# A later product, a later start and fewer one-hots on TensorE in the expert stage of a streaming-encoder trunk

## The chip, the cores and the metric

The kernel runs on one core of a Trainium2 chip. The metric is device time in microseconds (us), the median of several runs. The engines are TensorE (PE in the rows, its weight loads PEld), VectorE (DVE), ScalarE (ACT), GpSimd (POOL) and SyncE (SP, which here only issues DMAs).

## The reference, cut to what matters

One layer: a convolution group and a state-space group side by side, then cross-attention to a memory, then PEER, and a final RMSNorm. There are 256 tokens of width 2048, in two tiles (tt = 0 and 1) of 128. Only PEER is touched:

```
s1, i1 = top_k(q1 . keys1, 16);  s2, i2 = top_k(q2 . keys2, 16)
idx, g = the 16 best of the 256 sums (s1 + s2), softmax over them   # 8 heads: 128 experts a token
act = gelu(einsum("td,tkd->tk", xt, u_tab[idx]))                    # the "curve" is this gelu
out = einsum("tk,tkd->td", g * act, v_tab[idx])                     # "the gates' product": g * act
```

There are 128 x 128 experts; an expert's number is 128 * i1 + i2.

## The kernel before

PEER's inner product over 2048 columns is split. For the last 1280 columns the rows of `u_tab` are gathered: `dot` (L925) issues one gather on GpSimd into one of five buffers (L928) and one multiply-and-sum on VectorE (L930, tile `u`), 128 for each token tile, 256 in all. For the first 768 columns TensorE scores all experts (`dense`, L960) into tables W[0] (tile WA) and W[1] (WB, read as `by_token`), and the 128 scores that a token needs are taken out of its table with one-hot matrices. That is **settling** (`settle`, L1086). It works on 32 groups of four tokens in each tile, tile 0 first:

- `onehots` (L992): eight small matmuls (L999, tile d) and two ScalarE relus (L1006) make one-hots E and H.
- `select` (L1010): y = table x E on TensorE (L1016 for tile 0, L1019 for tile 1).
- `pick` (L1023): VectorE multiplies H by y (L1026), and four matmuls add the columns up into `more` (L1028). A group is picked LAG = 3 (tile 0) or 2 (tile 1) groups after its one-hots.
- `finish` (L909), once a tile: ScalarE copies `more` (L911), TensorE adds the gathered and the dense part and turns them (L913 and L914, tile ptc), ScalarE takes the gelu (L915, tile cT), VectorE multiplies by the gates (L918: the product), TensorE turns it back (L920), ScalarE stores `coef` (L921).
- `left` and `build` (L1031, L1047): the table is written again, now with the coefficients. `left` makes dr (L1035) and a one-hot L, either by a matmul and a relu (L1043, L1044) or by an is_equal on VectorE (L1039). `build` makes R = relu(dr) x cT on VectorE (L1051), and four matmuls give pw (L1054), which ScalarE copies into the table (L1055). Tile 0's groups 0 to 27 are built while tile 1 is picked. Its last four and all 32 of tile 1 come behind that, in a tail (L1157 to L1163).

Then the V stage (L1202 to L1223) multiplies both tables with `v_tab`, 128 blocks of matmuls (tile acc).

VectorE's order is written by hand (L1122): a dot is written, then `Pace` advances `settle` by SETTLE_RATE = 2.2 steps, a step being the code up to the next `yield`. Settling starts ahead of dot number SETTLE_AT. TensorE and ScalarE are ordered by a scheduler, and each engine runs its queue in order. In the tail the scheduler orders VectorE too.

`finish` of tile 0 stands in `settle` at its place (L1112), so its two `yield`s on either side of the product are steps of `settle`: four steps, of which two lie ahead of the product.

Of the kernel before, what the change touches and what calls it, by code (L numbers as in the profile page):

```python
# [62 lines left out]
ROUTE_RATE = 4.0  # L63
DENSE_RATE = 0.8
SETTLE_RATE = 2.2
SETTLE_AT = 176
FEATS_AT = 150
LAG = (3, 2)
DELAY = 16
# [9 lines left out]
def trunk(ctx, tc, a, out, dbg=None):  # L79
# [3 lines left out]
    def bc(ap, shape):  # L83
        return ap.to_broadcast(shape)
# [64 lines left out]
    with ExitStack() as wctx:  # L149
# [71 lines left out]
        def run(g):  # L221
            for _ in g:
                pass
# [763 lines left out]
    def feats(route, g):  # L987
        return fe_at[route.tt][:, g % 8], C[:, g // 8]
# [3 lines left out]
    def onehots(route, g):  # L992
        psq, lr_q = settling_pools
        f, cs = feats(route, g)
        one = []
        for s, nm in ((1, "E"), (0, "H")):
            d = psq.tile([P, 4, P], F32, name="d")
            for i in range(4):
                PE.matmul(d[:, i, :], cs[:, i, :], f[:, s, :], start=i == 0, stop=i == 3, skip_group_check=True)  # L999
            if nm == "E":  # L1000
                x = lr_q.tile([P, 4, P], F32, name="E")
            elif route.tt and g % 3 == 2:
                x = spare_h
            else:
                x = lr_q.tile([P, 4, P], F32, name="H", tag="R" if route.tt == 0 and g % 4 > 1 else "H")
            S.activation(x, d, AF.Relu)  # L1006
            one.append(x)
        return one

    def select(route, g, E, H):  # L1010
        psq, lr_q = settling_pools
        y = psq.tile([P, 4, P], F32, name="y", tag="dr" if route.tt == 0 and g % 4 > 1 else "y")
        for i in range(4):
            t = 4 * g + i
            if route.tt == 0:
                PE.matmul(y[:, i, :], W[0][:, t, :], E[:, i, :], start=i == 0, stop=i == 3, skip_group_check=True)  # L1016
            else:
                for h in range(2):
                    PE.matmul(y[64 * h:64 * h + 64, i, :], by_token[:, h, t, :], E[:, i, :], start=i == 0, stop=i == 3,  # L1019
                              skip_group_check=True)  # L1020
        return H, y

    def pick(route, g, H, y):  # L1023
        if g == 0:
            route.more = psu.tile([P, NSLOT], F32, name="more", bufs=1)
        V.tensor_mul(H, H, y)  # L1026
        for i in range(4):
            PE.matmul(route.more[i * NQ:(i + 1) * NQ, :], onecol[:, NQ - g:2 * NQ - g], H[:, i, :], start=g == 0,  # L1028
                      stop=g == NQ - 1)

    def left(route, g):  # L1031
        psq, lr_q = settling_pools
        f, cs = feats(route, g)
        dr = psq.tile([P, 4, P], F32, name="dr")
        PE.matmul(dr, f[:, 0, :], cs, start=True, stop=True)  # L1035
        tag, bufs = ("L", 3) if route.tt == 0 or g % 2 else ("H", 2)
        L = lr_q.tile([P, 4, P], F32, name="L", tag=tag, bufs=bufs)
        if route.tt and g % 2:
            V.tensor_tensor(L, bc(iota[:, None, :P], [P, 4, P]), bc(route.gT[:, 1, 4 * g:4 * g + 4, None], [P, 4, P]),  # L1039
                            op=ALU.is_equal)  # L1040
        else:
            d = psq.tile([P, 4, P], F32, name="d")
            PE.matmul(d, f[:, 1, :], cs, start=True, stop=True)  # L1043
            S.activation(L, d, AF.Relu)  # L1044
        return dr, L

    def build(route, g, dr, L):  # L1047
        psq, lr_q = settling_pools
        ts = slice(4 * g, 4 * g + 4)
        R = lr_q.tile([P, 4, P], F32, name="R", tag="E" if route.tt and g % 2 else "R", bufs=2)  # L1050
        V.scalar_tensor_tensor(R, dr, 0.0, bc(route.cT[:, ts, None], [P, 4, P]), op0=ALU.max, op1=ALU.mult)  # L1051
        pw = psq.tile([P, 4, P], F32, name="pw", tag="y") if route.tt and g % 2 else psu.tile([P, 4, P], F32, name="pw")
        for i in range(4):
            PE.matmul(pw[:, i, :], L[:, i, :], R[:, i, :], start=i == 0, stop=i == 3, skip_group_check=True)  # L1054
        S.copy(W[route.tt][:, :, ts], pw.rearrange("p t b -> p b t"))  # L1055

    routes = [Route(0), None]
# [28 lines left out]
    def settle():  # L1086
        groups = P // 4
        ones_at, held = {}, {}
        for tt in range(NTT):
            lefts = []  # L1090
            lag = LAG[tt]
            for n in range(groups + lag):
                if n < groups and (tt, n) not in ones_at:
                    ones_at[tt, n] = onehots(routes[tt], n)
                if 0 < n <= groups:
                    held[tt, n - 1] = select(routes[tt], n - 1, *ones_at.pop((tt, n - 1)))
                yield
                if n >= lag:
                    pick(routes[tt], n - lag, *held.pop((tt, n - lag)))
                    yield  # L1100
                if tt:
                    if HOLD < n <= groups:
                        build(routes[0], n - HOLD - 1, *lefts.pop())
                    if HOLD <= n <= groups:
                        lefts.append(left(routes[0], n - HOLD))
                    yield
            if tt == 0:
                while tick[0] <= NSLOT:
                    yield
                for n in range(2):  # L1110
                    ones_at[1, n] = onehots(routes[1], n)
                yield from routes[0].finish()  # L1112
            else:
                held_left.append(lefts.pop())

# [9 lines left out]
    for tt in range(NTT):  # L1125
        for g in range(len(GROUPS[tt])):
            while (tt, g) not in ready:
                next(routing)
            h0, n = routes[tt].heads(g)
            for j in range(h0 * TOPK, (h0 + n) * TOPK):  # L1130
                if tick[0] == SETTLE_AT:
                    run(routing)
                    run(dense_gen)
                    for _, task in tasks:
                        run(task)
                    psd_x.close()
                    lr_d_x.close()
                    settling_pools += [
                        psx.enter_context(tc.tile_pool(name="psq", bufs=2, space=PSUM, reuse_waits="tile")),
                        lr_x.enter_context(tc.tile_pool(name="lr_q", bufs=2, side="right", reuse_waits="tile"))]  # L1140
                    load_feats(1)
                    settling = settle()
                    paces = [Pace(settling, SETTLE_RATE)]
                routes[tt].dot(j)
                tick[0] += 1
                for at, task in tasks:
                    if tick[0] >= at:
                        next(task, None)
                if tick[0] == FEATS_AT:
                    load_feats(0)  # L1150
                for p in paces:
                    p()
    run(settling)
    order.close()
    finishing = routes[1].finish()
# [3 lines left out]
    for i, (tt, g) in enumerate(todo):  # L1159
        now, ahead = ahead, left(routes[todo[i + 1][0]], todo[i + 1][1]) if i + 1 < len(todo) else None  # L1160
        if tt == 1 and g == 0:
            run(finishing)
        build(routes[tt], g, *now)  # L1163
# [108 lines left out]
```

## Time and profile before

| | us |
|---|---|
| runs, median (lowest to highest of 3) | 2059.61 (2057.92 to 2060.23) |
| the profiled execution's own time | 2058.54 |
| its span, first to last instruction | 2056.8 |
| TensorE busy, share of the span | 1960.9 (95%) |
| VectorE busy | 1681.5 (82%) |
| ScalarE busy | 999.4 (49%) |
| GpSimd busy | 786.2 (38%) |

The profiled execution took 1.07 us less than the median, and 1.7 us of it lie outside the span. The shares are means over stages with different limits. The stages that matter here, in us from the span's start: dots beside the dense scores to 1292, settling of tile 0 to 1361, of tile 1 to 1478, the tail to 1525, the V stage to 2038, the final norm to the end. A TensorE that is busy all the time may still be stretched, since the ends of matmuls are modelled.

### The profile page before, as it was taken

The numbers are of one execution on the slowest core, as the hardware profiler recorded it, in microseconds if no ns is written. First come the engines' busy times: TensorE is split into PE (matmuls) and PEld (weight loads), VectorE is DVE, ScalarE is ACT, GpSimd is POOL, SyncE is SP. The second block draws the span as 40 slices with busy tenths as digits, with TensorE's granted clock in tenths as the row PEclk, the third lists the DMA queues.
The fourth block names the chain that finished last, engine by engine and source line by source line (L and its number), as shares of the span: only waits on it lengthen the run. The fifth ranks groups of instructions, "written<-read, shape, count | busy, mean of one in ns | idle before, by whom it ended". The sixth has DMA issues, their size and how long they took to land.

```text
span 2056.8 us, 33321 instructions
## 1 busy us (share of the span) xinstructions
PE 1960.9 (95%) x12361; PEld 1682.5 (82%) x12379; DVE 1681.5 (82%) x2757; ACT 999.4 (49%) x1586; POOL 786.2 (38%) x589
## 2 busy tenths in 40 slices
PE   7899999998999999999999999989999999999996
PEld 7888886786899888888888878867678888888885
DVE  6699999895665557999976667888869899899998
ACT  5775765454644445333333323556554444444444
POOL 1011111000000004443446655453128777677775
PEclk9999999999999999999999999999999999999998
DMA  8888788857855567999999999988539999999996
GB/s 245 198 226 222 202 220 227 229 179 221 286 174 177 168 203 266 305 312 321 322 363 403 408 390 396 302 289 266 160 143 337 359 339 336 346 339 336 342 339 226
DMA packets 203108, 571.78 MB, mean 278 GB/s; under 512 B 31410, under 2 KB 39459, under 8 KB 202818
## 3 DMA queue, kind: packets, MB, share of 16 engines
q1 hardware_dynamic: 135810, 307.48, 44.4%
q0 software_dynamic: 67136, 262.18, 38.0%
q8 instruction: 97, 1.59, 0.3%
q14 instruction: 65, 0.53, 0.1%
HBM read 556.74 MB, written 12.85 MB: 277 GB/s over the span
## 4 chain that ended last, share of the span: by engine, by line
PE 56%; DVE 15%; issue 11%; DMA 8%; POOL 7%; ACT 1%; SPq 0%; POOLq 0%; DVEq 0%; ACTq 0%
PE acc L1220 8%; PE acc L1219 8%; PE acc L1218 8%; POOL u L928 7%; DVE u L930 5%; PE mm L216 4%; PE mm L215 4%; PE mm L214 4%; PE mm L206 3%; PE mm L207 3%; PE mm L205 3%; PE pw L1054 3%; DMA w_lo<-in_w_kv_mem 3%; PE y L1019 1%; DMA xc<-in_mem 1%
## 5 line engine op out<-in xcount | busy, mean ns | idle before, releaser
L1183 POOL DMA_INDIRECT v<-in_peer_v,vidx x256 | 394.1, 1539 | 180.9 <-DVE accg L1185 70.5
L930 DVE SCALAR_TENSOR_TENSOR u<-u,hnF 128x1280 f32<-128x1280 f32 x256 | 384.5, 1505 | 81.5 <-DMA u<-in_peer_u,uidx 79.5
L928 POOL DMA_INDIRECT u<-in_peer_u,uidx x256 | 300.3, 1173 | 324.3 <-DVE u L930 235.6
L978 PE MATMUL sy<-hnT,ut 128*128 128x256 f32 x1536 | 357.5, 385 | 13.4 <-ACT ut L974 12.4
L191 ACT CAST w_hi<-w_raw 128x1024 fp32r<-128x1024 f32 (+2 forms) x228 | 231.4, 1017 | 246.1 <-PE mm L207 116.0
L978 PEld LDWEIGHTS sy<-hnT,ut 128*128 128x128 f32 x1536 | 287.2, 193 | 54.7 <-ACT ut L974 16.3
L196 DVE TENSOR_TENSOR w_lo<-w_raw,w_hi 128x1024 fp32r<-128x1024 f32 (+2 forms) x192 | 227.4, 1186 | 112.9 <-ACT w_hi L191 110.7
L103 ACT CAST vh<-vr 128x1472 fp32r<-128x1472 f32 x128 | 183.1, 1431 | 251.5 <-PE acc L1219 167.9
L1219 PE MATMUL acc<-vh,wl 128*128 128x512 f32 (+1 forms) x768 | 295.4, 385 | 0.0
L1220 PE MATMUL acc<-vl,wh 128*128 128x512 f32 (+1 forms) x768 | 293.7, 385 | 0.2 <-DVE vl L104 0.2
L216 PE MATMUL mm<-aT_hi,w_lo 128*128 128x256 f32 x960 | 270.6, 289 | 17.9 <-DMA w_lo<-in_w_in 6.8
L1218 PE MATMUL acc<-vh,wh 128*128 128x512 f32 (+1 forms) x768 | 275.9, 384 | 2.4 <-ACT vh L103 2.4
L214 PE MATMUL mm<-aT_hi,w_hi 128*128 128x256 f32 x960 | 276.2, 290 | 0.3 <-ACT w_hi L191 0.3
L215 PE MATMUL mm<-aT_lo,w_hi 128*128 128x256 f32 x960 | 273.8, 287 | 0.0
L104 DVE TENSOR_TENSOR vl<-vr,vh 128x1472 fp32r<-128x1472 f32 x128 | 216.7, 1693 | 45.5 <-ACT vh L103 34.7
L1185 DVE SCALAR_TENSOR_TENSOR accg<-v,coef,accg 128x576 f32<-128x576 f32 x256 | 208.6, 815 | 4.1
L216 PEld LDWEIGHTS mm<-aT_hi,w_lo 128*128 128x128 f32 x960 | 181.9, 193 | 24.4 <-DMA w_lo<-in_w_in 8.0
L214 PEld LDWEIGHTS mm<-aT_hi,w_hi 128*128 128x128 f32 x960 | 185.0, 193 | 5.8 <-issue 3.7
L215 PEld LDWEIGHTS mm<-aT_lo,w_hi 128*128 128x128 f32 x960 | 185.4, 193 | 3.4 <-issue 2.0
L974 ACT COPY ut<-ut 128x768 f32<-128x768 f32 x128 | 100.4, 800 | 168.0 <-PE ut L972 143.8
L1219 PEld LDWEIGHTS acc<-vh,wl 128*128 128x128 f32 x768 | 144.5, 188 | 30.6 <-DVE wl L1209 0.4
L1218 PEld LDWEIGHTS acc<-vh,wh 128*128 128x128 f32 x768 | 144.7, 188 | 28.3 <-ACT vh L103 2.6
(385 smaller groups left out, 3233.3 us busy)
## 6 DMA issues: line engine op xcount, KB each, us to landing
vr<-in_peer_v SPq DMA_DIRECT2D x128, 736.0 KB
raw<-in_peer_u SPq DMA_DIRECT2D x127, 384.0 KB
w_raw<-in_w_kv_mem SPq DMA_DIRECT2D x64, 512.0 KB
w_raw<-in_w_in SPq DMA_DIRECT2D x48, 512.0 KB
w_raw<-in_w_out SPq DMA_DIRECT2D x32, 512.0 KB
w_raw<-in_w_q_mem SPq DMA_DIRECT2D x32, 512.0 KB
w_raw<-in_w_o_mem SPq DMA_DIRECT2D x32, 512.0 KB
w_lo<-in_w_kv_mem POOLq DMA_DIRECT2D x24, 512.0 KB
```

The costliest lines, as they stand in the source:

```text
L191: S.copy(hi, raw)
L196: V.tensor_sub(lo, raw, hi.bitcast(F32))
L214: PE.matmul(o, wh, ah, start=first and cb % 2 == 0, stop=False, skip_group_check=True)
L215: PE.matmul(o, wh, al, start=False, stop=False, skip_group_check=True)
L216: PE.matmul(o, wl, ah, start=False, stop=last and end, skip_group_check=True)
L928: G.indirect_dma_start(out=u, out_offset=None, in_=a["peer_u"].rearrange("e (q c) -> (e q) c", c=GU), in_offset=bass.IndirectOffsetOnAxis( ...
L930: V.scalar_tensor_tensor(u, u, 1.0, hnF[:, self.tt, :], op0=ALU.mult, op1=ALU.mult, accum_out=self.act[:, j:j + 1])
L978: PE.matmul(ps[:, b % 2, :], ut[:, k, :], hnT[:, k, :], start=k == 0 and b % 2 == 0, stop=k == KD - 1 and b % 2 == 1, skip_group_check=True)
L1183: G.indirect_dma_start(out=v, out_offset=None, in_=table, in_offset=bass.IndirectOffsetOnAxis(ap=vidx[tt][:, j:j + 1], axis=0))
L1218: PE.matmul(o, wh[:, tt, :], vh[:, cs_], start=b == 0, stop=False)
L1219: PE.matmul(o, wl[:, tt, :], vh[:, cs_], start=False, stop=False)
L1220: PE.matmul(o, wh[:, tt, :], vl[:, cs_], start=False, stop=b == NB - 1)
```

## The change

Three edits. (1) In `settle`, only the first part of tile 0's `finish` stays at its place; the rest (product, turn back, `coef`) is run at the start of step n = 3 of tile 1, and its four yields are no longer steps of `settle`. (2) SETTLE_AT goes from 176 to 179. (3) In `left`, the groups of tile 1 whose one-hot L is made on VectorE are those with g % 3 not 0 (21 of 32) in place of the odd ones (16 of 32).

```diff
-SETTLE_AT = 176
+SETTLE_AT = 179
...
-        if route.tt and g % 2:
+        if route.tt and g % 3:
             V.tensor_tensor(L, bc(iota[:, None, :P], [P, 4, P]), bc(route.gT[:, 1, 4 * g:4 * g + 4, None], [P, 4, P]),
                             op=ALU.is_equal)
         else:
...
             for n in range(groups + lag):
+                if (tt, n) == (1, 3):
+                    run(finishing)
                 if n < groups and (tt, n) not in ones_at:
...
-                yield from routes[0].finish()
+                finishing = routes[0].finish()
+                next(finishing)
```

VectorE where tile 0 ends (L930 a dot, L1026 a pick's product, L918 the gates' product), as a difference:

```order
 L930 SCALAR_TENSOR_TENSOR u,act<-u,hnF 128x1280
 L1026 TENSOR_TENSOR H<-H,y 128x512
+L930 SCALAR_TENSOR_TENSOR u,act<-u,hnF 128x1280 x3
+L1026 TENSOR_TENSOR H<-H,y 128x512
 L930 SCALAR_TENSOR_TENSOR u,act<-u,hnF 128x1280
 L918 TENSOR_TENSOR cT<-cT,gT 128x128
-L930 SCALAR_TENSOR_TENSOR u,act<-u,hnF 128x1280 x3
-L1026 TENSOR_TENSOR H<-H,y 128x512
-L930 SCALAR_TENSOR_TENSOR u,act<-u,hnF 128x1280 x2
 L1026 TENSOR_TENSOR H<-H,y 128x512
 L930 SCALAR_TENSOR_TENSOR u,act<-u,hnF 128x1280
```

Three dots and tile 1's first pick now stand ahead of the product, and two dots fewer lie between the last pick of tile 0 and the second pick of tile 1.

TensorE at the same place (L914 and L920 the two turns of `finish`, L1028 a pick's matmuls, L1019 y of tile 1):

```order
 L914 MATMUL ptc<-ident,cT 128x128
-L920 MATMUL ptc<-ident,cT 128x128
 L1028 MATMUL more<-H,onecol 32x128 x4
 L1019 MATMUL y<-E,WB 64x128 x8
...
 L999 MATMUL d<-hnT,C 128x128
+L920 MATMUL ptc<-ident,cT 128x128
 L1028 MATMUL more<-H,onecol 32x128 x4
 L1019 MATMUL y<-E,WB 64x128 x8
```

The turn back, which waits for the product, moved behind tile 1's first pick and the next y and d.

VectorE in the tail, a piece of before and the like piece of now (R the product with cT, L the one-hot made by is_equal):

```order
L1051 SCALAR_TENSOR_TENSOR R_14241<-dr_14223,cT_14067 128x512
L1039 TENSOR_TENSOR L_14291<-iota_72,gT_10723 128x512
L1051 SCALAR_TENSOR_TENSOR R_14255<-dr_14237,cT_14067 128x512
L1051 SCALAR_TENSOR_TENSOR R_14267<-dr_14249,cT_14067 128x512
L1039 TENSOR_TENSOR L_14317<-iota_72,gT_10723 128x512
L1051 SCALAR_TENSOR_TENSOR R_14281<-dr_14263,cT_14067 128x512
```

Now:

```order
L1051 SCALAR_TENSOR_TENSOR R_14213<-dr_14195,cT_14067 128x512
L1039 TENSOR_TENSOR L_14261<-iota_72,gT_10723 128x512
L1051 SCALAR_TENSOR_TENSOR R_14225<-dr_14209,cT_14067 128x512
L1039 TENSOR_TENSOR L_14223<-iota_72,gT_10723 128x512
L1051 SCALAR_TENSOR_TENSOR R_14239<-dr_14221,cT_14067 128x512
L1039 TENSOR_TENSOR L_14287<-iota_72,gT_10723 128x512
L1051 SCALAR_TENSOR_TENSOR R_14251<-dr_14233,cT_14067 128x512
L1039 TENSOR_TENSOR L_14249<-iota_72,gT_10723 128x512
L1051 SCALAR_TENSOR_TENSOR R_14263<-dr_14247,cT_14067 128x512
L1051 SCALAR_TENSOR_TENSOR R_14277<-dr_14259,cT_14067 128x512
L1051 SCALAR_TENSOR_TENSOR R_14289<-dr_14271,cT_14067 128x512
```

Before, one L stood between every two R; now a cycle of six groups has six R and four L, each of the four between two R.

## Rows read from the trace of the kernel before

**Rows 1.** Stretch, length, busy us of PE, PEld, DVE, ACT, POOL; clock, DMA, GB/s.

```profile
1302.00:1355.00 53.00, 52.72 (x676) 43.42 (x674) 52.96 (x79) 31.26 (x56) 24.25 (x26) 1.00 0.91 312
1366.00:1380.00 14.00, 11.66 (x126) 8.37 (x127) 13.03 (x20) 5.76 (x10) 10.86 (x8) 0.74 0.93 324
1403.00:1470.00 67.00, 66.58 (x781) 48.58 (x790) 60.52 (x93) 42.63 (x75) 23.38 (x25) 1.00 0.82 250
1485.00:1518.00 33.00, 32.44 (x242) 27.89 (x247) 25.95 (x40) 21.17 (x39) 0.00 (x0) 1.00 0.00 1
```

**Rows 2.** VectorE in order of time, 1354 to 1380: start, us, what [idle before].

```profile
1354.16 1.48 DVE L930 SCALAR_TENSOR_TENSOR u<-u,hnF 128x1280 f32<-128x1280 f32 x1
...
1361.19 0.29 DVE L918 TENSOR_TENSOR cT<-cT,gT 128x128 f32<-128x128 f32 x1 [5.54 <-ACT cT L915]
1361.39 1.48 DVE L930 SCALAR_TENSOR_TENSOR u<-u,hnF 128x1280 f32<-128x1280 f32 x1
...
1362.81 1.49 DVE L930 SCALAR_TENSOR_TENSOR u<-u,hnF 128x1280 f32<-128x1280 f32 x1
...
1378.26 0.68 DVE L1026 TENSOR_TENSOR H<-H,y 128x512 f32<-128x512 f32 x1
1378.86 0.68 DVE L1051 SCALAR_TENSOR_TENSOR R<-dr,cT 128x512 f32<-128x512 f32 x1
```

**Rows 3.** TensorE in order of time, 1359 to 1382.

```profile
1359.62 0.69 PE L914 MATMUL ptc<-ident,cT 128*128 128x128 f32 x2
1361.53 0.33 PE L920 MATMUL ptc<-ident,cT 128*128 128x128 f32 x1 [1.23 <-DVE cT L918]
1366.46 0.65 PE L1028 MATMUL more<-H,onecol 128*32 128x128 f32 x8 [4.60 <-DVE H L1026]
...
1376.35 0.43 PE L1028 MATMUL more<-H,onecol 128*32 128x128 f32 x8 [1.07 <-DVE H L1026]
...
1381.21 0.43 PE L1028 MATMUL more<-H,onecol 128*32 128x128 f32 x8
```

**Rows 4.** ScalarE in order of time, at the gelu of tile 0.

```profile
1360.88 0.28 ACT L915 ACTIVATE cT<-ptc 128x128 f32<-128x128 f32 x1
```

**Rows 5.** VectorE in order of time, where settling starts.

```profile
1287.65 1.49 DVE L930 SCALAR_TENSOR_TENSOR u<-u,hnF 128x1280 f32<-128x1280 f32 x1 [0.84 <-DMA u<-in_peer_u,uidx]
...
1294.84 0.69 DVE L1026 TENSOR_TENSOR H<-H,y 128x512 f32<-128x512 f32 x1 [5.70 <-PE y L1016]
```

**Rows 6.** GpSimd in order of time, the gathers at the same place.

```profile
1280.70 2.12 POOL L928 DMA_INDIRECT u<-in_peer_u,uidx  x1 [0.30 <-issue]
...
1286.38 1.23 POOL L928 DMA_INDIRECT u<-in_peer_u,uidx  x1 [0.30 <-issue]
```

**Rows 7.** TensorE in order of time, where tile 1's settling ends.

```profile
1474.23 0.43 PE L1028 MATMUL more<-H,onecol 128*32 128x128 f32 x8
...
1476.73 0.38 PE L1043 MATMUL d<-C,hnT 128*128 128x512 bf16 x1 [0.69 <-ACT L L1044]
...
1478.19 1.16 PE L1054 MATMUL pw<-R,L 128*128 128x128 f32 x8 [0.21 <-ACT cT L915]
```

**Rows 8.** VectorE at the last dot, and in the tail.

```profile
1474.55 1.49 DVE L930 SCALAR_TENSOR_TENSOR u<-u,hnF 128x1280 f32<-128x1280 f32 x1
...
1506.90 0.69 DVE L1039 TENSOR_TENSOR L<-iota,gT 128x512 f32<-128x512 f32 x1 [0.53 <-PE pw L1054]
1507.51 1.41 DVE L1051 SCALAR_TENSOR_TENSOR R<-dr,cT 128x512 f32<-128x512 f32 x2
1509.44 0.69 DVE L1039 TENSOR_TENSOR L<-iota,gT 128x512 f32<-128x512 f32 x1 [0.53 <-PE pw L1054]
```

**Rows 9.** TensorE in the tail, in order of time.

```profile
1508.02 0.38 PE L1043 MATMUL d<-C,hnT 128*128 128x512 bf16 x1
1508.25 2.27 PE L1054 MATMUL pw<-R,L 128*128 128x128 f32 x16
```

**Rows 10.** Chain that ended last, by line, from 1540 to the end.

```profile
by line: PE acc L1219 32.2%; PE acc L1220 32.2%; PE acc L1218 32.0%; DVE accg L1185 0.7%; issue 0.5%; DVE WA L1240 0.3%; DVE WB L1240 0.3%; DVE WB L1228 0.3%; DVE WA L1228 0.2%; ACT WB L1230 0.2%; DVEq L1268 0.1%; DVE WB L1237 0.1%; DVE rms
```

## The prediction, made before the changed kernel ran

> **What bounds the kernel now.** I read the busy times by stage first, then each engine in order of time around the three edited places, and last the chain that ended last. By stage, settling of tile 0 keeps TensorE and VectorE both full, 52.7 and 53.0 of 53 us. In settling of tile 1 TensorE is full (66.6 of 67) and VectorE has some 10% left. In the tail TensorE again has the most, 32.4 of 33 [rows 1]. Between tile 0 and tile 1 lies a hole. VectorE, whose order is fixed, reaches the gates' product after the dot of 1354.16 and stands still for 5.54 us until the gelu has ended [rows 2, 4]. Behind the product stand three dots, and only then the first pick of tile 1, so TensorE is idle for 1.23 and 4.60 us [rows 3]. Its granted clock then is 0.74 on average from 1366 to 1380, though it has work there [rows 1]. After 1540 the chain is 96% matmuls of the V stage [rows 10], whose inputs are the finished tables: what the tables gain, the end gains.
>
> **The product, three groups later.** I write VectorE's queue down by hand with the spacings of the rows: 1.41 us a dot (1361.39 to 1362.81), 0.60 a pick or an R (1378.26 to 1378.86), 0.20 the product (1361.19 to 1361.39) [rows 2]. The dot of 1354.16 and two more end at 1358.4, the first pick of tile 1 at 1359.0, one dot at 1360.4. The gelu ends at 1361.16 as before, since nothing ahead of it moved [rows 4]; so a wait of 0.8 is left of 5.54. Product to 1361.4, second pick to 1362.0, a dot, third pick to 1364.0, two dots, fourth pick to 1367.4. TensorE can do its matmuls of the fourth pick at 1367.5 (before: 1376.35). What is queued behind the waiting product is the second pick, 1.0 us late at most, and on TensorE behind the turn back the second pick's matmuls, which wait for that same pick.
>
> From there TensorE is the slower one. Before, the fifth pick's matmuls start at 1381.21 [rows 3] and the last of tile 1, 27 groups later, at 1474.23 [rows 7]: 93.0 / 27 = 3.45 us a group. VectorE needs 3 steps / 2.2 = 1.36 dots, a pick and an R, 1.36 x 1.41 + 1.20 = 3.13. So the fifth pick's matmuls come at 1367.5 + 3.45 = 1370.9, 10.3 us earlier, and the lead stays, since dots, picks and builds keep their ratio. A second way: TensorE's idle time of 1.23 + 4.60, its 2.3 idle in the 14 us after 1366, and 14 x (1 - 0.74) = 3.6 lost to the clock make 11.8. Short gaps remain: from the third to the fourth pick's matmuls, 3.4 us apart now, TensorE has a group's 3.45 less the build's pw (1.1 for eight, half of the 2.27 in [rows 9]) and dr (0.2) to do, so it waits 1.3 there, and some 2 us in all. That makes 9.8. I take **10.0**. Below, the gain can't be less than the plain idle time less the 0.8 still waited for, 5.0; above, not more than 11.8.
>
> The clock is part of this. In the rows TensorE was idle for most of 1360 to 1366 and was granted 0.74 in the next 14 us; from 1403 to 1470 and in the tail, without such a hole, it was granted 1.00, that is 2.4 GHz rather than a mix with 1.2 [rows 1, 3]. The Trainium skill (TensorE: Matmul & The Clock Gate, What's actually happening) says that the clock has only these two levels and goes down after idleness and up again with work. Read against the new gaps, it leaves the sum as it is if they are too short to count, and leads to the second rival if they do count; no row decides it.
>
> **The start, three dots later.** VectorE idles 5.70 us ahead of the first pick of tile 0 [rows 5], and three more dots (4.2 us) now stand there. Their data: five buffers mean that the gather issued at 1280.70 fed the dot of 1287.65, which waited for it; that is 4.8 us after the issue ended at 1282.82. The third of the new dots is fed by the gather of 1286.38, whose issue ended at 1287.61 [rows 6]; so it has its data at about 1292.4 and ends at 1293.9, ahead of 1294.84. I cost the dots at 0 there. Without that cover the first pick, and with it the whole queue of a full VectorE, is up to 4.2 late. What they save is VectorE's time, which with the four steps gone keeps dots and steps ending together: 167 steps in 77 dots, where before 171 were spread over 80 and two dots were left over. The second of these started at 1474.55 [rows 8]; the turn of L913 needs it, and TensorE meanwhile waited twice for a buffer of a one-hot made ahead, 0.69 the second time [rows 7]. From the last pick's matmuls to the first pw took 1474.23 to 1478.19, 3.96 us. Now one dot is left there and one of the two waited-for one-hots moved behind the turn: 0.69 for that, and the one dot less gives the rest up to 1.41 + 0.69 = 2.1. I take **1.5**, between 0.5 and 2.1. The DMA queues of SP and GpSimd keep their order.
>
> **The tail.** Five matmuls of L1043 fall away, each 0.22 us from its start to the next start (1508.02 to 1508.25) [rows 9]: **1.1**. VectorE gets five more L of 0.6. Before, two groups took 2.54 us (1506.90 to 1509.44), of which VectorE waited 0.53 and worked 2.01 [rows 8]. Now six groups have ten instructions of 0.60 to 0.72, 6.0 to 7.0 us, against TensorE's 3 x 2.54 - 0.22 = 7.4: it still fits, though an L that waits for a buffer holds an R behind it. Bounds: 2.0 gained (if the waits for R go as well) and 2.0 lost. Against this term stands a row: in the tail weight loads fill only 27.9 of 33 us though matmuls fill 32.4 [rows 1]. The Trainium skill (Perfetto Trace Analysis, Identifying the Most-Contended Engine) says that matmul busy time is a poor measure of how full TensorE is, and weight-load busy time a good one. By that rule TensorE has room in the tail, the term would be 0, and the third rival below would hold. The 32.4 and the constant 2.54 us of two groups make me keep the 1.1.
>
> **Sum.** 10.0 + 1.5 + 1.1 = 12.6. The profiled execution took 2058.54, so 2045.9 by it; the median of the runs is 1.07 higher, so **2047.0**.
>
> **Rivals.**
> 1. TensorE was behind anyway and only the plain hole is won: after it, a group runs into VectorE's dots. 5.83 - 0.8 + 1.5 + 1.1 = 7.6, so 2052.0. For it: VectorE was full from 1366 to 1380 (13.0 of 14). Against: two dots fewer stand in that stretch.
> 2. The clock falls all the same, in the gaps between 1360 and 1367. The loss of 3.6 stays: 2050.6. For it: about 2 us of gaps in 7. Against: short gaps stand ahead of the tail too [rows 7], and the tail's clock is 1.00 [rows 1].
> 3. The tail's pace comes from the way through the engines (dr, R, pw, copy), not from TensorE's work, so that five matmuls less gain nothing: 12.6 - 1.1 = 11.5, so 2048.1. For it: weight loads at 85% of the stretch [rows 1]. Against: no other engine is over 80% there [rows 1].
> 4. Slower: the tail turns into VectorE's. Each of the 21 L waits for its buffer (0.53) and works 0.60 with an R behind it that TensorE then waits for: at most 21 x 1.13 = 23.7 lost, and 2047.0 + 1.1 + 23.7 = 2071.8. It decides once a one-hot costs TensorE 11.5 / 21 = 0.55, half of that; the time at three quarters is 2065.9. For it: L now stands between every two R for four groups in a row. Against: VectorE's 20% left.
> 5. The change doesn't do what it says: the wait at the product stays whole because the pick ahead of it waits for `more`, which `finish` must copy first. Against: the pick on VectorE (L1026) reads H and y alone; only its matmuls write `more`. If it holds, only 1.5 + 1.1 are won: 2057.0.
>
> **How the numbers follow.** Forecast 0.60 (its own range 2044.2 to 2049.5), first rival 0.12, second 0.10, third 0.07, fourth 0.05, fifth 0.06. The lower bounds of the three terms, 5.0 + 0.5 - 2.0 = 3.5, would give 2056.1, the upper ones, 11.8 + 2.1 + 2.0, 2043.7. The range of 2043.7 to 2053.5 leaves out the last two rivals and the worst of the dots' cover, under 0.2. About 0.2%, 4.1 us, is what a measurement of this kernel can tell from no change: faster, below 2055.5, is the forecast and the first three rivals, 0.89; within it the fifth and a little of the fourth, 0.07; slower the rest of the fourth, 0.04.
>
> **What would show it.** The product waits under 1.5 us; TensorE has no gap above 1.5 us between 1359 and 1372 and a clock of 1.00 there; the fifth pick's matmuls of tile 1 start about 1371; the first pick of tile 0 starts by 1295; the first pw of the tail lies 11 to 12 us earlier; 32 groups of the tail take 1 us less, and TensorE waits for R no more than before. A late first pick, a new gap behind the product, or a group above 1.3 us in the tail would make the prediction wrong.

## The result and the profile after

| | median us (runs) | before, same chip (runs) | ratio | 95% interval |
|---|---|---|---|---|
| changed kernel | 2049.59 (12) | 2061.89 (12) | 0.9936 | 0.9924 to 0.9949 |
| again | 2047.79 (6) | 2063.11 (29) | 0.9919 | 0.9894 to 0.9944 |
| a third time | 2047.88 (7) | 2060.70 (24) | 0.9940 | 0.9918 to 0.9961 |

The change makes the kernel faster: by the first ratio 13.2 us (10.5 to 15.7), where 12.6 was forecast. The rows below are from the third measurement's profile (span 2045.3 us); the first measurement's own profile is of a disturbed execution and is not used.

The work ahead of the edits ends at a different time in every execution: the first one-hot's matmul on TensorE (L999) starts between 1291.1 and 1303.4 us in the profiles here, whatever the kernel. So stages are compared from that start, F, on. It is 1292.01 before and 1292.98 here; times of the forecast are to be read 0.97 later.

Busy us by stretch (columns as in [rows 1]), the hole and the tail, each as far behind F or behind the second product as there:

```profile
1366.97:1380.97 14.00, 13.15 (x168) 9.94 (x167) 14.00 (x22) 8.06 (x15) 7.36 (x7) 1.00 0.94 312
1473.77:1506.77 33.00, 32.18 (x244) 28.42 (x247) 28.89 (x46) 19.88 (x36) 0.00 (x0) 1.00 0.00 1
```

TensorE went from 11.66 to 13.15 of 14 us and from a clock of 0.74 to 1.00. VectorE, with five more one-hots, is busy 28.89 of 33 us in the tail, 25.95 before [rows 1].

VectorE between the tiles, as [rows 2]:

```profile
1359.37 0.68 DVE L1026 TENSOR_TENSOR H<-H,y 128x512 f32<-128x512 f32 x1
1359.97 1.48 DVE L930 SCALAR_TENSOR_TENSOR u<-u,hnF 128x1280 f32<-128x1280 f32 x1
...
1362.39 0.29 DVE L918 TENSOR_TENSOR cT<-cT,gT 128x128 f32<-128x128 f32 x1 [0.93 <-ACT cT L915]
...
1368.03 0.68 DVE L1026 TENSOR_TENSOR H<-H,y 128x512 f32<-128x512 f32 x1
```

Of the wait of 5.54 us, 0.93 is left, and the first pick (1359.37) stands ahead of the product. TensorE at the same place, as [rows 3]:

```profile
1360.82 0.69 PE L914 MATMUL ptc<-ident,cT 128*128 128x128 f32 x2 [0.40 <-ACT cT L911]
...
1365.34 0.43 PE L1028 MATMUL more<-hnT,onecol 128*32 128x128 f32 x8 [0.24 <-DVE hnT L1026]
...
1368.77 0.43 PE L1028 MATMUL more<-H,onecol 128*32 128x128 f32 x8 [0.74 <-DVE H L1026]
...
1372.08 0.42 PE L1028 MATMUL more<-H,onecol 128*32 128x128 f32 x8
```

Where gaps of 1.23, 4.60 and 1.07 us stood, the gaps now are 0.40, 0.24 and 0.74. The fifth pick's matmuls start 79.10 us after F, before 89.20. The start of settling on VectorE, as [rows 5], and the end of tile 1 on TensorE, as [rows 7]:

```profile
1295.82 0.69 DVE L1026 TENSOR_TENSOR H<-H,y 128x512 f32<-128x512 f32 x1 [3.70 <-PE y L1016]
```

```profile
1464.47 0.43 PE L1028 MATMUL more<-H,onecol 128*32 128x128 f32 x8
...
1466.96 1.16 PE L1054 MATMUL pw<-R,L 128*128 128x128 f32 x8
```

VectorE still waits for TensorE ahead of the first pick, so here the three dots were free. From the last pick's matmuls to the first pw it takes 2.49 us, before 3.96. VectorE in the tail, as [rows 8]:

```profile
1501.44 0.69 DVE L1051 SCALAR_TENSOR_TENSOR R<-dr,cT 128x512 f32<-128x512 f32 x1 [0.41 <-PE dr L1035]
1502.33 0.69 DVE L1039 TENSOR_TENSOR L<-iota,gT 128x512 f32<-128x512 f32 x1 [0.20 <-PE pw L1054]
```

VectorE waits for dr and pw, that is for TensorE, as before. The V stage's first matmul of acc (L1221, before L1218) waits 2.39 us for vh as before, and the first one that needs vl starts 1.73 us behind it in both kernels. Before and now:

```profile
1527.22 0.70 PE L1218 MATMUL acc<-vh,wh 128*128 128x512 f32 x1 [2.39 <-ACT vh L103]
...
1528.95 0.80 PE L1220 MATMUL acc<-vl,wh 128*128 128x512 f32 x1 [0.18 <-DVE vl L104]
```

```profile
1515.03 0.50 PE L1221 MATMUL acc<-vh,wh 128*128 128x512 f32 x1 [2.39 <-ACT vh L103]
...
1516.76 0.50 PE L1223 MATMUL acc<-vl,wh 128*128 128x512 f32 x1 [0.77 <-DVE vl L104]
```

The longer wait for vl (0.77 for 0.18) costs nothing by itself, since vl comes no later. What differs is when the clock falls. The first 2 us of this stage and the next 4, before and then now (columns as in [rows 1]):

```profile
1527.22:1529.22 2.00, 1.82 (x4) 1.01 (x5) 2.00 (x4) 1.67 (x3) 1.76 (x1) 0.53 1.00 380
1529.22:1533.22 4.00, 4.00 (x15) 3.27 (x16) 1.68 (x2) 0.00 (x0) 3.14 (x3) 0.81 1.02 403
```

```profile
1515.03:1517.03 2.00, 1.23 (x4) 0.76 (x5) 2.00 (x4) 1.67 (x3) 1.76 (x1) 1.00 0.99 380
1517.03:1521.03 4.00, 4.00 (x12) 3.29 (x12) 1.68 (x2) 0.00 (x0) 3.15 (x3) 0.57 1.03 413
```

Before, it is low while TensorE would have waited for vl anyway. Now it is low behind that wait, and the first 24 matmuls of acc take 8.09 us, before 7.36.

Behind it the chain that ended last is matmuls of acc again, as [rows 10].

### The profile page after: what moved, and what is told of

It reads as the page before. It is cut to its first block, busy times and chain, and to the rows that moved or that the text cites. A ratio compares the mean times of both kernels' runs of the same rounds, so it can differ in the third digit from the quotient of the medians.

```text
span 7522.4 us, 33318 instructions
## 1 busy us (share of the span) xinstructions
PE 7481.8 (99%) x12357; PEld 5041.7 (67%) x12374; DVE 1704.9 (23%) x2762; ACT 1011.6 (13%) x1581; POOL 687.7 (9%) x589
## 3 DMA queue, kind: packets, MB, share of 16 engines
q0 software_dynamic: 67136, 262.18, 11.8%
## 5 line engine op out<-in xcount | busy, mean ns | idle before, releaser
L978 PE MATMUL sy<-hnT,ut 128*128 128x256 f32 x1536 | 1291.2, 1104 | 2.0 <-ACT ut L974 2.0
L214 PE MATMUL mm<-aT_hi,w_hi 128*128 128x256 f32 x960 | 869.5, 907 | 0.0
L215 PE MATMUL mm<-aT_lo,w_hi 128*128 128x256 f32 x960 | 858.6, 894 | 0.0
L216 PE MATMUL mm<-aT_hi,w_lo 128*128 128x256 f32 x960 | 849.8, 899 | 0.0
L1222 PE MATMUL acc<-vh,wl 128*128 128x512 f32 (+1 forms) x768 | 807.2, 1051 | 0.0
L1223 PE MATMUL acc<-vl,wh 128*128 128x512 f32 (+1 forms) x768 | 803.2, 1050 | 0.0
L214 PEld LDWEIGHTS mm<-aT_hi,w_hi 128*128 128x128 f32 x960 | 761.5, 794 | 34.3 <-issue 32.5
L215 PEld LDWEIGHTS mm<-aT_lo,w_hi 128*128 128x128 f32 x960 | 770.7, 803 | 18.4 <-issue 17.9
L1221 PE MATMUL acc<-vh,wh 128*128 128x512 f32 (+1 forms) x768 | 779.1, 1055 | 2.4 <-ACT vh L103 2.4
L216 PEld LDWEIGHTS mm<-aT_hi,w_lo 128*128 128x128 f32 x960 | 757.7, 800 | 22.6 <-issue 22.1
L1221 PEld LDWEIGHTS acc<-vh,wh 128*128 128x128 f32 x768 | 328.3, 428 | 274.7 <-issue 271.4
L930 DVE SCALAR_TENSOR_TENSOR u<-u,hnF 128x1280 f32<-128x1280 f32 x256 | 384.0, 1504 | 68.2 <-DMA u<-in_peer_u,uidx 63.4
```

The source lines that it names most:

```text
L214: PE.matmul(o, wh, ah, start=first and cb % 2 == 0, stop=False, skip_group_check=True)
L215: PE.matmul(o, wh, al, start=False, stop=False, skip_group_check=True)
L216: PE.matmul(o, wl, ah, start=False, stop=last and end, skip_group_check=True)
L930: V.scalar_tensor_tensor(u, u, 1.0, hnF[:, self.tt, :], op0=ALU.mult, op1=ALU.mult, accum_out=self.act[:, j:j + 1])
L978: PE.matmul(ps[:, b % 2, :], ut[:, k, :], hnT[:, k, :], start=k == 0 and b % 2 == 0, stop=k == KD - 1 and b % 2 == 1, skip_group_check=True)
L1221: PE.matmul(o, wh[:, tt, :], vh[:, cs_], start=b == 0, stop=False)
```

## The experiments

All stages from the profiles, in us: F to the matmuls of tile 1's fifth pick; the next 27 groups; the turn (last pick's matmuls to the second product on VectorE, L918); the tail (to the first matmul of acc); then to the end of the span; and the sum from F to the end against before. Settings are named by what they change in the kernel before. For the three edits: product, start, one-hots. Rate is SETTLE_RATE, and the filler is a row of unread matmuls in the hole; both come up below.

| kernel | 5th pick | 27 groups | turn | tail | V stage, end | sum - before | ratio of times (interval) |
|---|---|---|---|---|---|---|---|
| before | 89.2 | 93.0 | 3.95 | 49.05 | 529.6 | 0 | 1 |
| before, again | 89.4 | 93.0 | 3.95 | 49.05 | 529.5 | +0.1 | one run |
| all three, again | 79.5 | 92.4 | 2.47 | 48.09 | 530.3 | -12.0 | see above |
| all three, third time | 79.1 | 92.4 | 2.47 | 48.09 | 530.3 | -12.4 | see above |
| product | 79.2 | 95.3 | 6.38 | 51.58 | 530.1 | -2.1 | 0.9975 (0.9956 to 0.9994) |
| start | 88.9 | 93.4 | 2.19 | 49.04 | 529.4 | -1.8 | 0.9979 (0.9963 to 0.9995) |
| one-hots | 86.6 | 93.0 | 3.27 | 48.09 | 530.3 | -3.5 | 0.9974 (0.9959 to 0.9989) |
| product, start | 82.4 | 92.4 | 2.47 | 49.05 | 529.8 | -8.7 | 0.9952 (0.9931 to 0.9972) |
| product, rate 2.1 | 80.4 | 88.4 | 1.85 | 49.04 | 530.9 | -14.1 | 0.9945 (0.9923 to 0.9966) |
| filler | 86.5 | 90.4 | 3.95 | 49.04 | 531.5 | -3.4 | 0.9998 (0.9982 to 1.0015) |
| all three, rate 2.1 | 82.3 | 91.4 | 2.23 | 48.09 | 530.1 | -10.6 | 0.9942 (0.9923 to 0.9961) |
| product, one-hots, rate 2.1 | 81.0 | 88.5 | 1.85 | 48.09 | 533.6 | -11.7 | 0.9950 (0.9934 to 0.9966) |
| rate 2.1 | 85.5 | 87.2 | 2.28 | 49.07 | 530.9 | -9.7 | 0.9953 (0.9935 to 0.9970) |

The sums of the profiles lie in the intervals of the times (times some 2061) for all of them; where two kernels' intervals overlap, the table orders stages, not kernels.

**The changed kernel again**, without an edit.

> The changed kernel once more, for a profile at full clock. My theory: the product waits under 1.5 us, TensorE has no gap above 1.5 us between 1359 and 1372 and is granted about 1.00 there, the fifth pick of tile 1 comes at about 1371 (10 us earlier), the first pw of the tail 11 to 12 us earlier, the tail is 1.1 us shorter; time 12.6 us below before. Rival 1 (only the plain hole is won): the fifth pick comes 5 us earlier, 7.6 us in all. Rival 2 (the clock falls all the same): granted clock near 0.75 between 1366 and 1380, 9.0 us in all. Rival 3 (pace of the tail not set by TensorE): the tail as long as before, 11.5 us in all.

Measured: ratio 0.9919, and by stages 12.7 us less up to the first matmul of acc: 10.3 up to the last pick, 1.48 in the turn, 0.96 in the tail.

**One edit alone.** The product:

```diff
+                if (tt, n) == (1, 3):
+                    run(finishing)
...
-                yield from routes[0].finish()
+                finishing = routes[0].finish()
+                next(finishing)
```

> Before, with only the product moved three groups later (start and one-hots as before). My theory: the hole's 10 us are won, but settling now has 167 steps for 80 dots, so four dots are left over behind the last pick in place of two, and the turn that needs the last of them comes up to 2 x 1.41 = 2.8 us later: 7 to 9 us below before. Rival 1 (only the plain hole): 2 to 4 us. If the start is what matters: 0.

The start:

```diff
-SETTLE_AT = 176
+SETTLE_AT = 179
```

> Before, with only the start of settling three dots later. My theory: the three dots lie in the 5.7 us in which VectorE is idle, the hole at the product is as long as before (5.5 us), and with 171 steps for 77 dots none is left over behind the last pick: 1 to 2 us below before. Rival (the dots' data come late, or the start is worth more than the end): the first pick of tile 0 starts after 1296 and the time is up to 3 us above before.

The one-hots:

```diff
-        if route.tt and g % 2:
+        if route.tt and g % 3:
```

> Before, with only 21 one-hots of the tail on VectorE in place of 16. My theory: five matmuls of 0.22 us less on TensorE, which sets the tail's pace: 1.1 us below before. Rival 3: 0. Rival 4 (the tail turns into VectorE's): TensorE waits for R in most groups and the time is 2 us or more above before.

With the product alone the hole goes (fifth pick at 79.2), and then 7 of the 10 us are given back, so that 2.1 us are won by stages, where 7 to 9 were expected. Four steps fewer in `settle` mean that four dots stand behind the last pick. TensorE at the turn, and the stretch behind it (columns as in [rows 1]):

```profile
1475.71 0.76 PE L913 MATMUL ptc<-ident,act 128*128 128x128 f32 x2 [0.57 <-DVE u L930]
...
1477.33 2.07 PE L1054 MATMUL pw<-R,L 128*128 128x128 f32 x8 [0.43 <-ACT cT L915]
```

```profile
1471.38:1476.38 5.00, 2.81 (x8) 1.09 (x8) 4.19 (x7) 1.93 (x5) 0.00 (x0) 0.77 0.00 0
1476.38:1481.38 5.00, 3.90 (x17) 3.31 (x17) 0.98 (x2) 1.36 (x3) 0.00 (x0) 0.50 0.48 151
```

TensorE waits for the dots, is idle for nearly half of 5 us, and then gets a clock of 0.50, the lower of its two levels, so that the first eight pw take 2.07 us where they took 1.16. Turn and tail are 5.0 us longer, and the 27 groups 2.3 us, since the order of TensorE's queue is another (taken up with the slower feed). The start alone leaves the hole (its gap is 4.60 again) and shortens the turn by 1.76. The one-hots alone take 0.96 off the tail and 0.68 off the turn; their fifth pick at 86.6 is taken up below. So the edits are not independent: the start is what lets the product's gain reach the end.

**Product and start together, without the one-hots.**

> Product and start, one-hots of the tail as before. Counted from the first one-hot of settling to the first matmul of the V stage: before 235.2 us, changed kernel 222.5, product alone 232.5, start alone 233.5, one-hots alone 231.0 (of which 1.0 in the tail). Theory A (the two need each other: the product alone leaves four dots behind the last pick, and the hole there drops the clock in the tail): 222.5 + 1.0 = 223.5, no stretch of the tail below a clock of 1.00. Theory B (the parts add up): 235.2 - 2.7 - 1.7 = 230.8.

Groups and turn are those of the changed kernel, so with product and start there the third edit adds nothing to the turn. The tail is 0.96 longer, which is the one-hots' price once more. But the fifth pick is at 82.4, not 79.1, and the profile shows why, in VectorE where settling starts:

```profile
1298.08 1.56 DVE L930 SCALAR_TENSOR_TENSOR u<-u,hnF 128x1280 f32<-128x1280 f32 x1 [1.07 <-DMA u<-in_peer_u,uidx]
...
1300.86 1.49 DVE L930 SCALAR_TENSOR_TENSOR u<-u,hnF 128x1280 f32<-128x1280 f32 x1 [1.21 <-DMA u<-in_peer_u,uidx]
...
1303.41 1.49 DVE L930 SCALAR_TENSOR_TENSOR u<-u,hnF 128x1280 f32<-128x1280 f32 x1 [1.05 <-DMA u<-in_peer_u,uidx]
...
1304.83 0.68 DVE L1026 TENSOR_TENSOR H<-H,y 128x512 f32<-128x512 f32 x1
```

In this execution the three dots' rows came late. The first pick starts 7.56 us after F instead of 2.84, and 3.3 of the 4.7 are still there at the fifth pick. From F to the first matmul of acc it takes 226.3 us, and less these 3.3 it is 223.0, near Theory A. TensorE here has a gap of 1.85 us ahead of tile 1's first pick (1368.72), and the clock falls with it:

```profile
1368.20:1371.20 3.00, 2.48 (x24) 1.80 (x24) 3.00 (x6) 0.60 (x1) 2.39 (x3) 0.52 0.89 282
```

**Is it the low clock or VectorE's queue?** Kernel before with 22 matmuls whose result nobody reads, put on TensorE into the hole; VectorE's order stays, the scheduler's order of TensorE behind them changes a little:

```diff
-                yield from routes[0].finish()
+                finishing = routes[0].finish()
+                next(finishing)
+                wd = psu.tile([P, 4, P], F32, name="wd", tag="pw", bufs=1)
+                for _ in range(22):
+                    PE.matmul(wd, C[:, 0, 0], C[:, 0], start=True, stop=True)
+                yield
+                yield from finishing
```

> Before, with 22 extra matmuls of 0.22 us on TensorE whose result nobody reads, put in the hole behind the gelu (1361 to 1366), so that TensorE isn't idle there; the product's wait and VectorE's order stay. If the clock is a good part of the hole's price: granted clock at 1.00 in the 15 us behind the hole, and the fifth pick of tile 1 at 83.5 to 86 us from the first one-hot in place of 89.2 (86.6 and 88.9 in two other profiles of the same place); from the first one-hot to the V stage 230 to 233. If VectorE's late queue is the whole price: 89 and 235, whatever the clock. If the extra matmuls stand in the way: above 236.

and the kernel before again:

> The kernel before once more, for a second profile: whether the second fall of the clock, 85 to 90 us from the first one-hot, is there in each execution. The fifth pick of tile 1 at 89 with it, at 86.6 without it; all else in settling as in the first profile to 0.3 us.

TensorE with the filler (1377.56 is the fifth pick), and busy us by stretch (columns as in [rows 1]):

```profile
1360.23 4.91 PE L1116 MATMUL wd<-C 128*128 128x512 bf16 x22 [0.90 <-ACT cT L915]
...
1377.56 0.42 PE L1028 MATMUL more<-H,onecol 128*32 128x128 f32 x8
```

```profile
1361.06:1366.06 5.00, 4.94 (x32) 2.22 (x32) 5.00 (x8) 0.38 (x2) 3.27 (x3) 1.00 0.23 59
...
1376.06:1381.06 5.00, 5.00 (x65) 3.90 (x66) 4.86 (x8) 3.08 (x6) 1.88 (x2) 1.00 0.98 393
```

The same stretches of the kernel before, the last one of them in time a second fall of the clock:

```profile
1362.01:1367.01 5.00, 0.55 (x8) 0.23 (x8) 5.00 (x8) 0.15 (x1) 3.24 (x3) 0.65 0.23 46
1367.01:1372.01 5.00, 4.77 (x57) 3.37 (x57) 5.00 (x9) 1.98 (x4) 4.33 (x3) 0.67 0.93 312
1372.01:1377.01 5.00, 3.35 (x52) 2.21 (x53) 4.03 (x7) 2.75 (x6) 4.14 (x3) 1.00 0.99 383
1377.01:1382.01 5.00, 4.87 (x49) 4.02 (x47) 5.00 (x8) 2.47 (x5) 2.47 (x3) 0.66 0.90 296
```

And of the kernel with the one-hots alone, whose queues are those of before up to the turn:

```profile
1369.54:1374.54 5.00, 4.77 (x57) 3.43 (x57) 5.00 (x9) 2.04 (x4) 4.34 (x3) 0.68 0.91 323
1374.54:1379.54 5.00, 4.29 (x63) 2.96 (x60) 4.99 (x7) 3.12 (x6) 3.86 (x3) 1.00 0.92 330
1379.54:1384.54 5.00, 4.95 (x65) 3.94 (x64) 4.96 (x10) 2.95 (x6) 1.87 (x2) 1.00 0.97 365
```

With the clock at 1.00 all through, the fifth pick comes at 86.5. With the first fall but not the second it comes at 86.6 (one-hots alone), with both at 89.2 and 89.4 (before). So the first seems to cost nothing that lasts: VectorE is full there (5.00 of 5), and its dots pace the first picks.

The second fall doesn't stand alone. One-hots and before have the same queues up to the turn, and in both GpSimd had issued no gather for 6.3 us while VectorE stood at the product. But only in the kernel before does a dot ahead of the fourth pick then wait for its row (1.05 us in the second profile; the one-hots' profile shows no such wait):

```profile
1374.20 1.49 DVE L930 SCALAR_TENSOR_TENSOR u<-u,hnF 128x1280 f32<-128x1280 f32 x1 [0.97 <-DMA u<-in_peer_u,uidx]
```

The fourth pick's matmuls then start at 84.35 and 84.55 us after F, with the one-hots alone at 83.34; TensorE is idle ahead of them for 1.07 [rows 3] and 1.20 us, and the clock falls behind that. So of the 2.6 and 2.8 us, 1.0 and 1.2 are the late row's, and the other 1.6 lie between the fourth and the fifth pick: 4.86 and 4.85 us at the low clock, 3.26 without. The start alone, where the clock fell a second time too, has 2.17 us idle ahead of the fourth pick.

Both theories of the expectation were too simple. The filler's ratio, 0.9998, shows no gain; its profile was the fastest of its ten runs.

**A slower feed.** In the run with product and rate 2.1 the start stayed at 176:

```diff
-SETTLE_RATE = 2.2
+SETTLE_RATE = 2.1
```

> Product three groups later, settling starting at dot 176 as before, but 2.1 steps a dot in place of 2.2: 167 steps in 80 dots, so that no more than one dot is left behind the last pick. Theory A (what the start gives beside the product is that dots and steps end together): the clock stays at 1.00 in the tail; tile 0 becomes some 2 us longer, since it has 30.5 dots in place of 29, and the stretch from the first one-hot to the V stage takes 224 to 227 us. Theory C (the start gives its gain by filling VectorE's idle 5.7 us): 231 to 233, as for the product alone.

It does better than any theory had it: 219.7 us from F to the first matmul of acc. The turn is 1.85, so slowing the feed does what the later start does, and a group takes 88.4 / 27 = 3.27 us. That was followed up with four kernels on one chip: the changed kernel,

> The changed kernel once more, beside the three below. Theory A (the three terms add up to 12.7 us from the first one-hot to the first matmul of the V stage): ratio near 0.993, that stretch 222 to 223.5 us. Rival T (the clock dips after the hole now and then, so that the stretch was lucky in the profile before): 225 or more, with a stretch of clock under 0.8 between 60 and 100 us after the first one-hot.

all three edits with rate 2.1,

> The changed kernel with SETTLE_RATE 2.1 in place of 2.2. Theory A (a slower feed of picks lets TensorE's queue stand in another order with 3.25 us a group in place of 3.42, as in the run with product and rate): 27 groups x 0.17 = 4.6 us less, so 218 us from the first one-hot to the first matmul of the V stage and about 2043 us. Rival C (dots end before the picks do: 167 steps at 2.1 take 79.5 dots and only 77 are left, so that steps without dots stand at the end, VectorE has less to do there and TensorE paces as before): 221 to 223 us, no gain. Rival L (the 3.25 was chance of that one queue): 222.5 or more.

the same with the start at 176,

> The changed kernel with SETTLE_RATE 2.1 and the start at dot 176 again: the run with product and rate plus the tail's edit. Theory A (terms add up): 219.7 of that run less 1.0 for the tail, 218.7 us from the first one-hot to the first matmul of the V stage, and 1.0 us less than its time. Rival L (the queue's order was chance): 222 us or more.

and rate 2.1 alone:

> The kernel before with SETTLE_RATE 2.1 alone, so the product stays where it was. Theory A (the hole is the product's, the shorter group the rate's): VectorE still waits about 5.5 us at the product and TensorE has a gap over 4 us, the fifth pick of tile 1 at 86 to 89 us after the first one-hot, then 3.25 us a group: 229 to 231 us to the first matmul of the V stage, and 2055 us. Rival R (the rate by itself takes the hole away, by moving picks nearer to the dots): the wait under 2 us, 220 to 224 us, 2049 us. Rival L: no shorter group, 234 to 235 us.

The changed kernel's stages came again within 0.5 us. All three with rate 2.1 missed Theory A's 218 us (224.1, as Rival L had it). With the start at 176 Theory A held by stages (219.4 for 218.7), but not in the times. Rate 2.1 alone gains 9.7 us (0.0047 x 2060.7; 6.2 to 13.4) with the hole still there. TensorE in that kernel, at the hole and 54 us later:

```profile
1366.79 0.65 PE L1028 MATMUL more<-H,onecol 128*32 128x128 f32 x8 [4.60 <-DVE H L1026]
...
1424.39 0.43 PE L1028 MATMUL more<-H,onecol 128*32 128x128 f32 x8
1424.75 1.09 PE L1019 MATMUL y<-E,WB 128*64 128x128 f32 x16
```

and in the kernel before:

```profile
1432.23 0.42 PE L1028 MATMUL more<-H,onecol 128*32 128x128 f32 x6
1432.58 0.40 PE L999 MATMUL d<-hnT,C 128*128 128x128 bf16 x4
1432.91 0.41 PE L1028 MATMUL more<-H,onecol 128*32 128x128 f32 x2
1433.25 0.40 PE L999 MATMUL d<-hnT,C 128*128 128x128 bf16 x4
```

Theory A's 229 to 231 us fell (224.1 measured), though TensorE's gap and its 3.25 us a group (3.23) were there: the second fall of the clock stayed away and the turn went to 2.28. Rival R's times all but came (224.1 for 220 to 224, 2049.4 for 2049), but not its mechanism: the gap stayed, and VectorE still waited 2.89 us at the product, though not 5.5.

The group is shorter with next to no idle time on TensorE on either side (1.0 and 0.9 us in 27 groups). The trace shows two reasons in the order of the queue. In 7 of the 27 groups before, a pick's matmuls are broken by d: 0.35 and 0.34 from start to next start, where unbroken they take 0.36. That is 0.33 us in such a group, 2.3 in all. And a bf16 matmul takes 0.09 us longer to the next start when one of the narrow matmuls of pick or y (128*32, 128*64) stands behind it than when a full-width one (128*128) does. Before, and then with the rate alone:

```profile
1406.64 0.38 PE L1043 MATMUL d<-C,hnF 128*128 128x512 bf16 x1
1406.95 1.09 PE L1019 MATMUL y<-E,WB 128*64 128x128 f32 x16
```

```profile
1407.47 0.38 PE L1043 MATMUL d<-C,hnF 128*128 128x512 bf16 x1
1407.68 0.39 PE L999 MATMUL d<-hnT,C 128*128 128x128 bf16 x4
```

There are 49 such changes in the 27 groups before. With the rate alone there are 27, since y follows its pick directly in 26 of 27 groups; 22 x 0.09 = 2.0 us. Together 4.3 of the 5.8 us; the rest stays open. The product alone has 9 broken picks and 53 changes, the changed kernel 5 and 49.

Rate 2.1 on top of the change gains nothing that can be told: ratios 0.9942 and 0.9950 beside 0.9940. The one with the start at 176 has the shortest stretch of all, 219.4 us, and gives 3.4 us of it back in the V stage. Its TensorE and, behind it, its VectorE there:

```profile
1530.25 0.50 PE L1222 MATMUL acc<-vh,wl 128*128 128x512 f32 x1 [4.15 <-DVE wl L1212]
```

```profile
1522.69 0.82 DVE L1188 SCALAR_TENSOR_TENSOR accg<-v,coef,accg 128x576 f32<-128x576 f32 x1 [2.48 <-DMA v<-in_peer_v,vidx]
1526.71 1.67 DVE L1188 SCALAR_TENSOR_TENSOR accg<-v,coef,accg 128x576 f32<-128x576 f32 x2 [3.21 <-DMA v<-in_peer_v,vidx]
...
1529.91 0.28 DVE L1212 TENSOR_TENSOR wl<-WA,wh 128x128 fp32r<-128x128 f32 x1
```

VectorE waits for gathered rows that the V stage's queue has ahead of wl, and TensorE waits for wl. No kernel tried is shown to beat the changed one.

## Why the prediction was right, point by point

**The sum.** 12.6 us forecast; 13.2 (10.5 to 15.7) in the times, 12.4 and 12.0 by stages. The 2047.0 itself stands beside 2049.59 (just outside the forecast's own 2049.5, inside the whole range), 2047.79 and 2047.88; the kernel before ran 1 to 3.5 us above the 2059.61 that it started from.

**The product, 10.0.** Up to the last pick 10.7 and 10.3 were gained. The queue written by hand holds nearly to the row. With the 0.97 added, it has the first pick end at 1359.97 (row: the next dot starts at 1359.97), the product wait 0.8 (0.93), the fourth pick end at 1368.4 (1368.63), and the fifth pick's matmuls at 1371.87 (1372.08). Some 2 us of short gaps were expected, and the three shown make 1.38. TensorE's clock was 1.00. In the second profile the product waited 0.07.

That the size came out is in part luck. The row of 1381.21, from which the 10.3 us were counted, holds the late gathered row and the second fall of the clock, 2.6 us that an execution of the same order could do without. Beside that one (one-hots alone, 86.6) the fifth pick would have gained 7.5 us, not 10.1. Both profiles of the kernel before hold these 2.6 us; how many of its runs do isn't known.

The step "the lead stays" held for a weaker reason than was given. 3.45 us a group was read as what TensorE needs. It is what TensorE needs in that order of its queue: 3.42 here, 3.53 with the product alone, 3.23 with the rate alone. Nothing in the working excluded such a shift. With the product alone it cost 2.3 us, and the four dots left behind the last pick cost another 5.0 in turn and tail.

The second way, 11.8, counted 3.6 us for the clock as if a low clock were lost time, and its 2.3 idle us hold the 1.07 behind the late row. By the runs above the first fall costs little or nothing behind VectorE's dots, and the second, in the kernel before, 1.6. The Trainium skill (TensorE: Matmul & The Clock Gate, What's actually happening) has the clock go down after idleness and up again with work. The falls during 4.60 us idle and at the product-alone turn agree with it (0.65 and 0.50). So does the second fall, to 0.66: it follows a stretch in which TensorE was busy 3.35 of 5 us, with the one-hots alone 4.29. The length of a gap doesn't decide it by itself: gaps of 1.37 us in the changed kernel's second profile and of 1.89 with all three and rate 2.1 passed at 1.00.

**The start and the end, 1.5.** 1.48 and 1.48, and product and start without the third edit give the same turn. The three dots cost nothing in two profiles of the changed kernel (in the second, VectorE's idle time ahead of the first pick was just used up) and in two more with the start at 179. In the fifth they did, 4.7 us at the first pick and 3.3 at the fifth, near the 4.2 that was named as the price without cover. The 5.70 us of idle time that cover them is one execution's. In the other profiles with the start at 176 it is 3.1 to 10.6 us.

**The tail, 1.1.** 0.96, in all five profiles with these one-hots, and the kernel with product and start lacks just that. VectorE took its five L. There, TensorE's weight loads of pw waited for R 6 times (2.2 us in all), before 13 times (4.4 us). So no third and no fourth rival. Weight loads fill 28.42 of 33 us there, 86%. The Trainium skill (Perfetto Trace Analysis, Identifying the Most-Contended Engine) judges TensorE's room by weight loads, and by the share of peak work, which no run here gives. The prediction read from this that the term would be 0, which was too much: by weight loads, too, TensorE was the fullest engine of the tail before, 27.89 of 33 us beside VectorE's 25.95 [rows 1], and five matmuls fewer moved the end.

**What was left out.** The V stage took 0.7 us longer (530.3 twice for 529.6), since the clock falls later in it: what the tables gain, the end gains, less that. That this about evens out what the product gained above its 10.0 is luck. The first rival's mechanism showed only without the later start: the product alone runs into VectorE's dots, at the end of tile 1, and wins 2.1. The second's, a fall of the clock in the new gaps, showed once, where the dots' rows came late (product and start, 0.52). The fifth fell, since the first pick does not wait for `more` (1359.37, ahead of the product).

## What to carry to other kernels

Where an engine's order is fixed, write its queue down with start-to-start spacings of the trace: each start here came out within 0.3 us. Look for waits of the feeding engine inside the row that a gain is counted from, and in a second profile: 2.6 of the 10 us stood there by one late gather and the fall of the clock behind it. Before believing that a gain stays, ask what pace the engine behind it would take in another order, and try the one constant that sets the feed: rate 2.1 alone reached most of this three-part change. Count stages from an event of the program, since the part ahead of the edits moved by 12 us between executions, as much as the change is worth.

## What was not expected of the hardware

- After the same 4.60 us gap TensorE's clock fell a second time in three profiles (before, before again, the start alone) and not in two others (one-hots, rate). In the three, TensorE had been idle again for 1.07, 1.20 and 2.17 us ahead of the fourth pick; in the two others no gap at that place was above 0.47. The fall itself cost 1.6 us in the kernel before.
- The race between gathered rows and dense scores ahead of settling ended between 10.6 us early and 4.7 us late for VectorE, in kernels that do not differ there but for three dots.
- The same matmuls of a group took 3.23 to 3.53 us, with TensorE shown busy nearly throughout: what stands behind a matmul changes what it takes (0.31 us ahead of a narrow one, 0.21 ahead of a full-width one).
- After 2.39 us idle ahead of the V stage the clock fell at once before the change and some 2 us later with it, and with the later fall the first 24 matmuls there took 0.7 us longer.
